# Two of the four weight sums of a seven-product matrix multiply move to a GpSimd DMA, and all eight chunks use seven products

## The chip, the cores and the metric

The kernel runs on one core of one Trainium2 chip. The metric is the device time of one execution in microseconds (us); runs are compared by their medians. The core has a matrix engine (TensorE: PE for its matmuls, PEld for its weight loads), a vector engine (VectorE, DVE), a scalar engine (ScalarE, ACT), GpSimd (POOL), and SyncE (SP), which here only issues DMAs. Each engine works through its own instructions in order and waits at an instruction until the semaphores it needs have been set.

## The reference

Two layers work on 256 tokens of width 2048 in float32: a recurrent block with a feed-forward network (FFN), then a block of sliding-window attention with an FFN. The change is in the FFN:

```python
D_FF = ((8 * D_MODEL // 3 + 255) // 256) * 256     # 5632

def swiglu_ffn(x, g, w_in, w_out):
    h = rms_norm(x, g)
    gate, up = jnp.split(h @ w_in, 2, axis=-1)
    return x + (jax.nn.silu(gate) * up) @ w_out
```

## The kernel before, in words

**Jobs.** All weights come from DRAM in tiles of 128 x 1024 float32 (512 KB), 704 of them. One tile is one job: SP loads it into a buffer `raw` (four of them, used in turn), it is split into a rounded part `hi` and a remainder `lo` (four buffers each), and PE multiplies with both parts: three matmuls (high by high, low by high, high by low) stand for one float32 product. ACT makes `hi` (L363), DVE makes `lo` = `raw` - `hi` (L364). `stream` (L385) writes the program job by job: at job i it issues the load of job i + LD (4), the split of job i + LC (3), and the matmuls of job i. Between, it lets background tasks write their instructions, as long as counters of DVE's and ACT's work (`run_bg`) leave room. At build time a scheduler of the framework puts each engine's instructions in their final order, so they can stand in another order than they were written.

**The FFN's first multiply** has 22 groups of eight jobs (chunks of 256 rows of the weights) per layer. Groups 0 to 3 and the odd ones from 5 to 21 are ordinary: 24 matmuls of 256 columns a job. Groups 4, 6, ..., 20 (`FAST`, nine per layer, 18 in all) are fast groups: a chunk is a 2 x 2 block product, done with seven block products in place of eight, 21 matmuls in place of 24 (`fast`, L588). For that, sums of blocks of the weights are needed: `mix` (L366) makes `hi` and `lo` of three of the four 256-column blocks (L374, L379) and, in a buffer `d` of 128 x 1024, four sums: two by one DVE subtraction over 512 columns (L375), one more by L376, one more by L377. `d` is then split into `mh` (ACT, L378) and `ml` (DVE, L380). Seven of the eight chunks are done so (`PAIRS`); chunk 3 is done by `plain` (L573) with 24 matmuls and an ordinary split. `joined` (L742) puts the partial products of a fast group together, applies silu, and multiplies; `turn` transposes the result on PE (L765).

**What is kept.** A gated result is 128 x 512 (256 KB); 22 per layer stay in SBUF until `split` (L676) divides them into high and low parts for the FFN's second multiply. Working buffers of 128 x 1024 come from a pool of 37 (`WORK`); part of x is parked in DRAM during the FFN (`park`, `fetch`).

Of the kernel before, what the change touches and what calls it, by code (L numbers as in the profile page):

```python
# [17 lines left out]
P = 128  # L18
# [31 lines left out]
class Trunk:  # L50
    LD = 4
    LC = 3
# [12 lines left out]
    FAST = tuple(range(4, 21, 2))  # L65
    PAIRS = (0, 1, 2, 4, 5, 6, 7)
    EVEN = (0, 4)
    OWED = 9000.0
    BUSY = 780.0
    WORK = 37  # L70
    NEAR = 7
    MORE = 2800.0
    WARM = 30
# [3 lines left out]
    def __init__(self, ctx, tc, dram):  # L77
# [12 lines left out]
        const.tile([P, PAD], F32, name="pad")  # L90
        self.raw = [const.tile([P, 1024], F32, name=f"raw{i}") for i in range(4)]
        self.hi = [const.tile([P, 1024], F32R, name=f"hi{i}") for i in range(4)]
# [25 lines left out]
        self.started = False  # L118
        self.jobs = []
        self.mixed = {}  # L120
        self.pend = deque()
# [214 lines left out]
    def load(self, i):  # L336
        dma = self.nc.sync.dma_start
        raw, src = self.raw[i % 4], self.jobs[i][0]
        if i == 0:

            self.nc.scalar.dma_start(self.x[0][:, 0:2, :], self.d["x"][:, 0:2, :])
            self.nc.scalar.dma_start(self.par, self.d["par"])
            for h in range(2):
                dma(raw[:, 512 * h:512 * h + 512], src[:, 512 * h:512 * h + 512])
            dma(self.x[0][:, 2:4, :], self.d["x"][:, 2:4, :])
        else:
            dma(raw, src)
            if i in self.XLOAD:
                n = self.XLOAD[i]
                dma(self.x[n], self.d["x"][:, 4 * n:4 * n + 4, :])  # L350
                self.got = n
        if i == 4:
            dma(self.con, self.d["con"])

    def split(self, i):
        raw, hi, lo = self.raw[i % 4], self.hi[i % 4], self.lo[i % 4]
        if self.jobs[i][2]:
# [3 lines left out]
        for c in range(0, 1024, n):  # L361
            q = slice(c, c + n)
            self.nc.scalar.activation(hi[:, q], raw[:, q], AF.Copy)  # L363
            self.nc.vector.tensor_tensor(lo[:, q], raw[:, q], hi[:, q].bitcast(F32), ALU.subtract)  # L364

    def mix(self, i, raw, hi, lo):  # L366

        act, tt = self.nc.scalar.activation, self.nc.vector.tensor_tensor
        d = self.double(F32, True)
        near = self.jobs[i][2] == 1  # L370
        mh, ml = self.double(near=near), self.double(near=near)
        two = lambda ap: ap.rearrange("p (a c) -> p a c", c=T)
        q = slice(T, 4 * T)
        act(hi[:, q], raw[:, q], AF.Copy)  # L374
        tt(two(d[:, 0:2 * T]), two(raw[:, T:3 * T]), raw[:, 0:T].unsqueeze(1).to_broadcast([P, 2, T]), ALU.subtract)  # L375
        tt(d[:, 2 * T:3 * T], raw[:, 2 * T:3 * T], d[:, 0:T], ALU.add)  # L376
# [8 lines left out]
    def stream(self):  # L385
        n = len(self.jobs)
        for i in range(-self.LD, n):
            self.tick = 2 * i
            if i + self.LD < n:
                self.load(i + self.LD)  # L390
            if 0 <= i + self.LC < n:
                self.split(i + self.LC)
# [169 lines left out]
    def fast_group(self, src, xn, mx, g, done, final):  # L562
# [3 lines left out]

        def put(h, x, w, n=1):
            b = h // 2
            nc.tensor.matmul(st["ps"][b][:, h % 2 * T:(h % 2 + n) * T], x, w, start=b not in st["begun"], stop=True,  # L569
                             skip_group_check=True)  # L570
            st["begun"].add(b)

        def plain(c, hi, lo):  # L573

            x2 = [self.need(xn[2 * c + kt]) for kt in range(2)]
            wide = []
            for kt in range(2):
                for i in range(2):
                    xh, xl = (x2[kt][:, q * T + i * P:q * T + i * P + P] for q in range(2))
                    for x, w in ((xh, hi), (xl, hi), (xh, lo)):  # L580
                        wide.append((2 - 2 * i, x, w[:, kt * 2 * T:kt * 2 * T + 2 * T]))
            todo = [(h + e, x, w[:, e * T:e * T + T]) for h, x, w in wide for e in range(2)]
            for k, t in enumerate(todo):
                if k == len(todo) // 2:
                    self.half_tick()
                put(*t)

# [24 lines left out]
        for c in range(8):  # L612
            def mm(hi, lo, c=c):
                if c == 0:
                    st["ps"] = self.bank4()
                if c == self.EVEN[1]:
                    self.flush()
                (fast if c in self.PAIRS else plain)(c, hi, lo)
                if c == 7:
                    done(st["ps"])  # L620
            self.jobs.append((src(c), mm, (c in self.PAIRS) + (c in self.EVEN)))

# [5 lines left out]
    def ffn(self, l, xs, r, gains, rn, col, out=None):  # L628
# [47 lines left out]
        def split():  # L676
            for p in range(NH // 2):
                while not raws[p].ready:
                    yield 1
# [13 lines left out]
        def raw(g, s):  # L693
            raws[g].ap = s
            raws[g].ready = True

        for g in range(NH // 2):
# [44 lines left out]
            def joined(q, g=g):  # L742
# [6 lines left out]
                self.tt(two(part(1, 2)), two(at(6, 2)), twice(part(0)), ALU.add)  # L749
                self.tt(part(0), at(7), part(1), ALU.add)  # L750
                self.tt(c[:, 0:2 * T], at(0, 2), part(0, 2), ALU.add)
                self.tt(c[:, 2 * T:4 * T], at(2, 2), part(2, 2), ALU.add)
# [654 lines left out]
```

## Time and profile before

| | us |
|---|---|
| median of three runs (1970.23 to 1973.72) | 1971.62 |
| the profiled execution, its own time | 1970.22 |
| its span | 1968.4 |
| an ordinary group beside a fast one: 192 matmuls | 21.76 |
| the fast group after it: 171 matmuls and 4 transposes | 20.02 |

The span is what the profiler saw from the first to the last instruction; 1.8 us of the execution lie around it. Durations in a view are of one instruction from its start to its end; on one engine the next often starts a little before. A view of waits names the engine that waits, and behind the arrow what ended the wait. A view of windows gives for a stretch of time each engine's busy time, the granted clock, the share of time in which the 16 DMA engines moved packets, and GB/s.

### The profile page before, as it was taken

How to read it: one execution, taken by the hardware profiler on the slowest of the kernel's cores; microseconds unless marked ns; L12 is line 12 of the kernel's file. 1: busy time of each engine (PE TensorE's matmuls, PEld its weight loads, DVE VectorE, ACT ScalarE, POOL GpSimd, SP SyncE). 2: the span in 40 equal slices, each digit the busy share in tenths (PEclk: the TensorE clock that was granted, in tenths of full speed). 3: DMA queues.
4: the chain of work that ended last, by engine and by line, in shares of the span. 5: the costliest groups of instructions: out<-in, count | busy, mean ns of one | idle time of the engine just before them, and what ended most of it. 6: DMA issues, size and time to landing. Idle time of an engine off the chain costs nothing. (4 is left out here: it accounts for less than half of the span.)

```text
span 1968.4 us, 40256 instructions
## 1 busy us (share of the span) xinstructions
PE 1960.3 (100%) x16518; PEld 1920.3 (98%) x16518; DVE 1541.0 (78%) x2477; ACT 1144.2 (58%) x1672; POOL 0.2 (0%) x4
## 2 busy tenths in 40 slices
PE   9999999999999999999999999999999999999999
PEld 9999999999999999999998789999999999999999
DVE  7999868999899997554667776699899988954443
ACT  6798756555555566444566675565555555744442
POOL 0000000000000000000000000000000000000000
PEclk9999999999999999999999999999999999999999
DMA  8555665566656657656554335656666665666663
GB/s 281 183 192 177 218 215 193 176 212 205 211 196 204 204 200 244 196 187 202 194 182 145 123 119 170 208 186 201 201 204 203 203 214 196 235 204 204 205 204 128
DMA packets 107321, 384.97 MB, mean 196 GB/s; under 512 B 11904, under 2 KB 14080, under 8 KB 107136
## 3 DMA queue, kind: packets, MB, share of 16 engines
q1 hardware_dynamic: 106848, 381.99, 58.7%
q8 instruction: 129, 2.11, 0.4%
q14 instruction: 56, 0.46, 0.1%
q10 hardware_dynamic: 288, 0.40, 0.1%
HBM read 376.06 MB, written 6.29 MB: 194 GB/s over the span
## 5 line engine op out<-in xcount | busy, mean ns | idle before, releaser
L411 PE MATMUL b<-s,hi 128*128 128x256 f32 (+1 forms) x7958 | 1060.0, 280 | 1.4 <-ACT s L135 1.2
L411 PEld LDWEIGHTS b<-s,hi 128*128 128x128 f32 x7958 | 987.5, 188 | 13.2 <-ACT s L135 2.1
L364 DVE TENSOR_TENSOR lo<-raw,hi 128x1024 fp32r<-128x1024 f32 (+1 forms) x579 | 702.6, 1220 | 320.2 <-ACT hi L363 312.7
L363 ACT ACTIVATE hi<-raw 128x1024 fp32r<-128x1024 f32 (+1 forms) x579 | 608.1, 1056 | 469.8 <-PE b L411 405.4
L411 PE MATMUL b<-s,lo 128*128 128x256 f32 x4096 | 607.0, 276 | 0.0
L411 PEld LDWEIGHTS b<-s,lo 128*128 128x128 f32 x4096 | 530.3, 188 | 0.2
L378 ACT ACTIVATE s<-s 128x1024 fp32r<-128x1024 f32 x126 | 131.8, 1058 | 189.1 <-DVE s L377 189.0
L569 PE MATMUL b<-s,s 128*128 128x256 f32 x1512 | 195.9, 279 | 0.0
L569 PEld LDWEIGHTS b<-s,s 128*128 128x128 f32 x1512 | 183.0, 189 | 0.0
L569 PE MATMUL b<-hi,s 128*128 128x256 f32 x1044 | 178.0, 277 | 0.0
L380 DVE TENSOR_TENSOR s<-s,s 128x1024 fp32r<-128x1024 f32 x126 | 153.7, 1220 | 6.0 <-ACT s L378 5.9
L569 PEld LDWEIGHTS b<-hi,s 128*128 128x128 f32 x1044 | 152.3, 188 | 0.0
L569 PE MATMUL b<-lo,s 128*128 128x256 f32 x522 | 132.5, 276 | 0.0
L375 DVE TENSOR_TENSOR s<-raw 128x512 f32<-128x512 f32 x126 | 86.6, 687 | 43.5 <-DMA raw<-in_ffn_in 43.5
L379 DVE TENSOR_TENSOR lo<-raw,hi 128x768 fp32r<-128x768 f32 x126 | 118.6, 952 | 0.0
L135 ACT ACTIVATE s<-s 128x512 fp32r<-128x512 f32 (+3 forms) x176 | 87.6, 525 | 48.8 <-DVE s L144 36.9
L374 ACT ACTIVATE hi<-raw 128x768 fp32r<-128x768 f32 x126 | 102.1, 832 | 9.1 <-ACT s L378 4.9
L569 PEld LDWEIGHTS b<-lo,s 128*128 128x128 f32 x522 | 92.7, 188 | 0.0
L1295 PE MATMUL b<-hi,s 128*128 128x512 f32 x256 | 83.5, 406 | 0.0
L144 DVE TENSOR_TENSOR s<-s,s 128x512 fp32r<-128x512 f32 (+2 forms) x143 | 75.3, 557 | 3.9 <-ACT s L135 3.9
L135 ACT ACTIVATE s<-b 128x256 fp32r<-128x256 f32 (+4 forms) x134 | 58.9, 468 | 26.3 <-PE b L1269 6.7
L144 DVE TENSOR_TENSOR s<-b,s 128x512 f32<-128x512 f32 (+3 forms) x126 | 63.4, 533 | 5.3 <-ACT s L135 4.0
(115 smaller groups left out, 1112.9 us busy)
## 6 DMA issues: line engine op xcount, KB each, us to landing
raw<-in_ffn_in SPq DMA_DIRECT2D x352, 512.0 KB, 3.4
raw<-in_ffn_out SPq DMA_DIRECT2D x176, 512.0 KB, 4.2
raw<-in_lru_in SPq DMA_DIRECT2D x63, 512.0 KB, 4.0
raw<-in_lru_out SPq DMA_DIRECT2D x32, 512.0 KB, 3.3
raw<-in_w_q SPq DMA_DIRECT2D x32, 512.0 KB, 3.2
raw<-in_w_o SPq DMA_DIRECT2D x32, 512.0 KB, 3.6
raw<-in_gate SPq DMA_DIRECT2D x8, 512.0 KB, 4.1
away<-s SPq DMA_DIRECT2D x8, 512.0 KB, 3.2
```

Source lines behind the costliest of these rows:

```text
L135: self.nc.scalar.activation(out, in_, func, **kw)
L144: self.nc.vector.tensor_tensor(out, a, b, op)
L363: self.nc.scalar.activation(hi[:, q], raw[:, q], AF.Copy)
L364: self.nc.vector.tensor_tensor(lo[:, q], raw[:, q], hi[:, q].bitcast(F32), ALU.subtract)
L374: act(hi[:, q], raw[:, q], AF.Copy)
L375: tt(two(d[:, 0:2 * T]), two(raw[:, T:3 * T]), raw[:, 0:T].unsqueeze(1).to_broadcast([P, 2, T]), ALU.subtract)
L378: act(mh[:, :], d[:, :], AF.Copy)
L379: tt(lo[:, q], raw[:, q], hi[:, q].bitcast(F32), ALU.subtract)
L380: self.mark = tt(ml[:, :], d[:, :], mh[:, :].bitcast(F32), ALU.subtract)
L411: self.nc.tensor.matmul(ps[f][:, 0:c1 - c0], w, x2[k][:, c0:c1], start=f not in begun, stop=last and all(q[1] != f for q in todo[n + 1:]))
L569: nc.tensor.matmul(st["ps"][b][:, h % 2 * T:(h % 2 + n) * T], x, w, start=b not in st["begun"], stop=True, skip_group_check=True)
L1295: nc.tensor.matmul(st[g][b][:, :], x, q, start=c + kt == 0 and x is xh and q is wh, stop=c == 7 and kt == 1 and q is wl)
```

## The change

- A fifth `raw` buffer (`LP` = 5), and loads written six jobs ahead (`LD` = 6).
- `PAIRS` holds all eight chunks, `plain` is gone, so each fast group has 168 matmuls.
- Two of the four sums are no longer made by DVE's L375. A new step `two_sums`, written five jobs ahead of the matmuls and so two jobs ahead of `mix`, has ACT write the negated first block twice into `d`, and GpSimd issue a DMA that adds 512 columns of `raw` onto it.
- `joined` does without the sum that only `plain` needed.
- Gated results 8 to 13 of each layer are stored to DRAM by SP and loaded again when `split` is six results ahead of their use: 12 stores and 12 loads of 256 KB in all.
- The pool has 36 working buffers in place of 37; the planner's entry for a mixed chunk's DVE work, `MORE`, is 2200 in place of 2800.

```diff
-    LD = 4
+    LD = 6
+    LP = 5
...
-    PAIRS = (0, 1, 2, 4, 5, 6, 7)
+    PAIRS = tuple(range(8))
     EVEN = (0, 4)
+    ASIDE = tuple(range(8, 14))
...
-    WORK = 37
+    WORK = 36
     NEAR = 7
-    MORE = 2800.0
+    MORE = 2200.0
...
+    def two_sums(self, i):
+
+        if not self.jobs[i][2]:
+            return
+        raw, d = self.raw[i % self.LP], self.double(F32)
+        two = lambda ap: ap.rearrange("p (a c) -> p a c", c=T)
+        self.a(two(d[:, 0:2 * T]), raw[:, 0:T].unsqueeze(1).to_broadcast([P, 2, T]), scale=-1.0)
+        self.nc.gpsimd.dma_start(d[:, 0:2 * T], raw[:, T:3 * T], accum_op=ALU.add)
+        self.begun[i] = d
+
     def mix(self, i, raw, hi, lo):
 
         act, tt = self.nc.scalar.activation, self.nc.vector.tensor_tensor
-        d = self.double(F32, True)
+        d = self.begun.pop(i)
         near = self.jobs[i][2] == 1
         mh, ml = self.double(near=near), self.double(near=near)
-        two = lambda ap: ap.rearrange("p (a c) -> p a c", c=T)
         q = slice(T, 4 * T)
         act(hi[:, q], raw[:, q], AF.Copy)
-        tt(two(d[:, 0:2 * T]), two(raw[:, T:3 * T]), raw[:, 0:T].unsqueeze(1).to_broadcast([P, 2, T]), ALU.subtract)
         tt(d[:, 2 * T:3 * T], raw[:, 2 * T:3 * T], d[:, 0:T], ALU.add)
...
             if i + self.LD < n:
                 self.load(i + self.LD)
+            if 0 <= i + self.LP < n:
+                self.two_sums(i + self.LP)
             if 0 <= i + self.LC < n:
                 self.split(i + self.LC)
...
-                (fast if c in self.PAIRS else plain)(c, hi, lo)
+                fast(c, hi, lo)
...
         def split():
             for p in range(NH // 2):
+                if p + 6 in self.ASIDE:
+                    q = p + 6
+                    s = raws[q].ap = self.slot(F32)
+                    nc.sync.dma_start(s, self.away[l, q][:, :])
+                    raws[q].ready = True
...
         def raw(g, s):
             raws[g].ap = s
             raws[g].ready = True
+            q = g - 2
+            if q in self.ASIDE:
+                away = self.away[l, q] = self.dram.tile([P, 2 * T], F32, name=f"aside{l}_{q}")
+                nc.sync.dma_start(away[:, :], raws[q].ap)
+                self.free(raws[q].ap)
+                raws[q].ready = False
...
                 self.tt(two(part(1, 2)), two(at(6, 2)), twice(part(0)), ALU.add)
-                self.tt(part(0), at(7), part(1), ALU.add)
-                self.tt(c[:, 0:2 * T], at(0, 2), part(0, 2), ALU.add)
+                self.tt(c[:, 0:T], at(7), part(1), ALU.add)
+                self.tt(c[:, T:2 * T], at(1), part(1), ALU.add)
```

What this does to the order of instructions is shown at three places of the second layer, each in one pair of an ordinary and a fast group. The number behind `raw` names one of its buffers (73 to 76 before, 73 to 77 now), that behind `hi` and `lo` one of theirs; `s` with a number is one use of a working buffer.

ACT before, from the middle of an ordinary group on: the splits of the ordinary jobs (`hi` of 1024 columns, L363), then of the fast group's first chunks (`hi` of 768 columns, L374), between them the `mh` (`s`<-`s`, L378).

```order
L363 ACTIVATE hi_78<-raw_74 128x1024
L363 ACTIVATE hi_79<-raw_75 128x1024
L363 ACTIVATE hi_80<-raw_76 128x1024
L378 ACTIVATE s_15559<-s_15558 128x1024
L374 ACTIVATE hi_77<-raw_73 128x768
L378 ACTIVATE s_15594<-s_15593 128x1024
L374 ACTIVATE hi_78<-raw_74 128x768
L378 ACTIVATE s_15629<-s_15628 128x1024
L374 ACTIVATE hi_79<-raw_75 128x768
L135 ACTIVATE h_92<-b_146 128x256
L363 ACTIVATE hi_80<-raw_76 128x1024
L135 ACTIVATE h_91<-b_147 128x256
```

ACT now, at the same place: the negated copies (`s`<-`raw`, L138) of the first four chunks, the ordinary splits (L366), the first three `mh` (L389) and the `hi` of the first two chunks (L386).

```order
L138 ACTIVATE s_15666<-raw_76 128x512
L366 ACTIVATE hi_79<-raw_73 128x1024
L366 ACTIVATE hi_80<-raw_74 128x1024
L138 ACTIVATE s_15696<-raw_77 128x512
L389 ACTIVATE s_15729<-s_15666 128x1024
L138 ACTIVATE s_15726<-raw_73 128x512
L366 ACTIVATE hi_81<-raw_75 128x1024
L138 ACTIVATE s_15762<-raw_74 128x512
L386 ACTIVATE hi_78<-raw_76 128x768
L389 ACTIVATE s_15765<-s_15696 128x1024
L389 ACTIVATE s_15801<-s_15726 128x1024
L386 ACTIVATE hi_79<-raw_77 128x768
```

The copy of a chunk stands two to three jobs ahead of its `hi`, and the third chunk's copy stands behind the first chunk's `mh`.

DVE before, at that place: the sums of the first three chunks (L375, L376, L377), two ordinary `lo` (L364), the first `lo` of the fast group (L379) and two `ml` (L380).

```order
L375 TENSOR_TENSOR s_15558<-raw_73 128x512
L364 TENSOR_TENSOR lo_83<-raw_75,hi_79 128x1024
L376 TENSOR_TENSOR s_15558<-raw_73,s_15558 128x256
L377 TENSOR_TENSOR s_15558<-raw_73,s_15558 128x256
L375 TENSOR_TENSOR s_15593<-raw_74 128x512
L376 TENSOR_TENSOR s_15593<-raw_74,s_15593 128x256
L364 TENSOR_TENSOR lo_84<-raw_76,hi_80 128x1024
L380 TENSOR_TENSOR s_15560<-s_15558,s_15559 128x1024
L377 TENSOR_TENSOR s_15593<-raw_74,s_15593 128x256
L375 TENSOR_TENSOR s_15628<-raw_75 128x512
L379 TENSOR_TENSOR lo_81<-raw_73,hi_77 128x768
L380 TENSOR_TENSOR s_15595<-s_15593,s_15594 128x1024
```

DVE now: L387 and L388 are the two sums that are left to it, L367 and L390 the `lo` of ordinary and fast jobs, L391 the `ml`.

```order
L387 TENSOR_TENSOR s_15666<-raw_76,s_15666 128x256
L388 TENSOR_TENSOR s_15666<-raw_76,s_15666 128x256
L367 TENSOR_TENSOR lo_84<-raw_74,hi_80 128x1024
L391 TENSOR_TENSOR s_15730<-s_15666,s_15729 128x1024
L387 TENSOR_TENSOR s_15696<-raw_77,s_15696 128x256
L367 TENSOR_TENSOR lo_85<-raw_75,hi_81 128x1024
L388 TENSOR_TENSOR s_15696<-raw_77,s_15696 128x256
L387 TENSOR_TENSOR s_15726<-raw_73,s_15726 128x256
L388 TENSOR_TENSOR s_15726<-raw_73,s_15726 128x256
L390 TENSOR_TENSOR lo_82<-raw_76,hi_78 128x768
L391 TENSOR_TENSOR s_15766<-s_15696,s_15765 128x1024
L391 TENSOR_TENSOR s_15802<-s_15726,s_15801 128x1024
```

The 512-column subtraction is gone from each chunk. L387 now waits for the GpSimd DMA of its chunk, and the `lo` of an ordinary job (L367) can stand behind it.

DVE before, in the second half of the same fast group: sums, `lo` and `ml` of its last four chunks.

```order
L380 TENSOR_TENSOR s_15693<-s_15691,s_15692 128x1024
L379 TENSOR_TENSOR lo_81<-raw_73,hi_77 128x768
L379 TENSOR_TENSOR lo_82<-raw_74,hi_78 128x768
L380 TENSOR_TENSOR s_15725<-s_15723,s_15724 128x1024
L375 TENSOR_TENSOR s_15755<-raw_75 128x512
L379 TENSOR_TENSOR lo_83<-raw_75,hi_79 128x768
L376 TENSOR_TENSOR s_15755<-raw_75,s_15755 128x256
L375 TENSOR_TENSOR s_15790<-raw_76 128x512
L377 TENSOR_TENSOR s_15755<-raw_75,s_15755 128x256
L376 TENSOR_TENSOR s_15790<-raw_76,s_15790 128x256
L377 TENSOR_TENSOR s_15790<-raw_76,s_15790 128x256
L380 TENSOR_TENSOR s_15757<-s_15755,s_15756 128x1024
```

DVE now, in the second half of the fast group, from the sixth chunk's L387 on (buffer raw_76, which the first chunk had before it); the two L147 are halves of an earlier ordinary group's gated result.

```order
L387 TENSOR_TENSOR s_15838<-raw_76,s_15838 128x256
L147 TENSOR_TENSOR s_15648<-h_93,b_144 128x256
L388 TENSOR_TENSOR s_15838<-raw_76,s_15838 128x256
L390 TENSOR_TENSOR lo_85<-raw_74,hi_81 128x768
L147 TENSOR_TENSOR s_15648<-h_91,b_145 128x256
L391 TENSOR_TENSOR s_15875<-s_15798,s_15874 128x1024
L390 TENSOR_TENSOR lo_82<-raw_75,hi_78 128x768
L387 TENSOR_TENSOR s_15871<-raw_77,s_15871 128x256
L388 TENSOR_TENSOR s_15871<-raw_77,s_15871 128x256
L390 TENSOR_TENSOR lo_83<-raw_76,hi_79 128x768
L391 TENSOR_TENSOR s_15908<-s_15838,s_15907 128x1024
L390 TENSOR_TENSOR lo_84<-raw_77,hi_80 128x768
```

Five more rows end the group: the seventh chunk's `ml`, then L387, `lo`, L388 and `ml` of the eighth. Behind them stand four L367 in a row, the first four jobs of the next ordinary group, the fourth of them from raw_77, the buffer that is loaded next with the first chunk of the next fast group. The fourth chunk's `lo` (from raw_74) now stands behind the sixth chunk's sums, and so behind a wait for the sixth chunk's DMA.

More of the change, by code (lines that the diff above doesn't have):

```diff
@@ L90, in __init__ @@
         const.tile([P, PAD], F32, name="pad")
-        self.raw = [const.tile([P, 1024], F32, name=f"raw{i}") for i in range(4)]
+        self.raw = [const.tile([P, 1024], F32, name=f"raw{i}") for i in range(self.LP)]
         self.hi = [const.tile([P, 1024], F32R, name=f"hi{i}") for i in range(4)]
@@ L119, in __init__ @@
         self.jobs = []
+        self.begun = {}
         self.mixed = {}
@@ L337, in load @@
         dma = self.nc.sync.dma_start
-        raw, src = self.raw[i % 4], self.jobs[i][0]
+        raw, src = self.raw[i % self.LP], self.jobs[i][0]
         if i == 0:
@@ L355, in split @@
     def split(self, i):
-        raw, hi, lo = self.raw[i % 4], self.hi[i % 4], self.lo[i % 4]
+        raw, hi, lo = self.raw[i % self.LP], self.hi[i % 4], self.lo[i % 4]
         if self.jobs[i][2]:
@@ L565, in fast_group, with put @@
         st = {"begun": set()}
-        def put(h, x, w, n=1):
+        def put(h, x, w):
             b = h // 2
-            nc.tensor.matmul(st["ps"][b][:, h % 2 * T:(h % 2 + n) * T], x, w, start=b not in st["begun"], stop=True,
+            nc.tensor.matmul(st["ps"][b][:, h % 2 * T:h % 2 * T + T], x, w, start=b not in st["begun"], stop=True,
                              skip_group_check=True)
             st["begun"].add(b)
[L573 to L586, printed above, removed]
         def fast(c, hi, lo):
@@ L617, in mm @@
                     self.flush()
-                (fast if c in self.PAIRS else plain)(c, hi, lo)
+                fast(c, hi, lo)
                 if c == 7:
                     done(st["ps"])
-            self.jobs.append((src(c), mm, (c in self.PAIRS) + (c in self.EVEN)))
+            self.jobs.append((src(c), mm, 1 + (c in self.EVEN)))
     def flush(self):
```

## The prediction

> **What bounds the kernel now.** I read the page's list of busy times first, then the chain that ended last in one pair of groups, then the stage of the fast groups by windows.
>
> ```profile
> span 1968.4 us, 40256 instructions
> PE 1960.3 (100%) x16518; PEld 1920.3 (98%) x16518; DVE 1541.0 (78%) x2477; ACT 1144.2 (58%) x1672; POOL 0.2 (0%) x4
> ...
> 1369.61 21.76 PE b L411 x192
> 1391.37 9.96 PE b L569 x87
> 1401.33 0.44 PE b L765 x4
> 1401.77 9.62 PE b L569 x84
> ...
> 1391.37:1703.80 312.43, 312.43 (x2746) 312.43 (x2746) 286.95 (x396) 183.11 (x220) 0.00 (x0) 1.00 0.61 203
> ...
> DVE s L375 <- DMA raw<-in_ffn_in: 16.1, 16, 2.1
> ```
>
> PE is idle for 8.1 us in all. In a pair, PE's own work is the whole chain: 192 matmuls in 21.76 us, then 171 in 9.96 + 9.62 us and 0.44 for four transposes, 41.77 us a pair. The window from the second pair's fast group to the end of the stage holds 7.5 pairs: PE busy throughout, at the full granted clock (1.00). But DVE is busy 286.95 of 312.43 us, 38.3 us a pair, and waited 16.1 us more, 2.1 a pair, for weights. So PE is the bound by a narrow margin: the stage has two engines near their limit. That settles the reading: what comes off PE counts in full, as long as DVE and its suppliers keep up.
>
> **What PE loses.** Chunk 3 of each fast group goes from 24 matmuls to 21, and the order of the program has 54 matmuls fewer (3 x 18). One is (9.96 + 9.62) / 171 = 0.1145 us, so 54 x 0.1145 = **6.2 us**. Nothing else on PE changes but a few places of single small matmuls.
>
> **What DVE and ACT gain or lose.**
>
> ```profile
> L364 DVE TENSOR_TENSOR lo<-raw,hi 128x1024 fp32r<-128x1024 f32 x577 | 701.3, 1222 | 316.3 <-ACT hi L363 308.9 <-PE b L569 4.4
> L380 DVE TENSOR_TENSOR s<-s,s 128x1024 fp32r<-128x1024 f32 x126 | 153.7, 1220 | 6.0 <-ACT s L378 5.9
> L379 DVE TENSOR_TENSOR lo<-raw,hi 128x768 fp32r<-128x768 f32 x126 | 118.6, 952 | 0.0
> L375 DVE TENSOR_TENSOR s<-raw 128x512 f32<-128x512 f32 x126 | 86.6, 687 | 43.5 <-DMA raw<-in_ffn_in 43.5
> L377 DVE TENSOR_TENSOR s<-raw,s 128x256 f32<-128x256 f32 x126 | 53.1, 421 | 1.7
> L144 DVE TENSOR_TENSOR s<-b,s 128x512 f32<-128x512 f32 x54 | 35.4, 684 | 0.5
> ...
> L363 ACT ACTIVATE hi<-raw 128x1024 fp32r<-128x1024 f32 x577 | 606.8, 1057 | 468.0 <-PE b L411 405.4 <-PE b L1295 15.6 <-DMA raw<-in_ffn_in 13.2
> L378 ACT ACTIVATE s<-s 128x1024 fp32r<-128x1024 f32 x126 | 131.8, 1058 | 189.1 <-DVE s L377 189.0
> L374 ACT ACTIVATE hi<-raw 128x768 fp32r<-128x768 f32 x126 | 102.1, 832 | 9.1 <-ACT s L378 4.9 <-ACT hi L374 3.4 <-PE b L411 0.4
> L135 ACT ACTIVATE s<-s 128x512 fp32r<-128x512 f32 x74 | 44.9, 624 | 23.3 <-DVE s L144 16.2 <-DVE s L148 6.6
> ```
>
> Per pair DVE loses seven L375 (7 x 0.687 = 4.8 us), and a 512-column sum of `joined` becomes one of 256 (0.26). Chunk 3 turns from one L364 (1.22) into 0.95 + 1.22 + 2 x 0.42 = 3.01, which costs 1.8. Net -3.3: 35.0 us of work in a pair that PE would run in 41.4. So DVE may idle 6.4 us a pair. ACT gets eight negated copies of 512 columns (I take L135's 0.62, the same size) and 0.83 us for chunk 3: 24.4 us a pair become 30.2, hidden as long as the copies do not stall it.
>
> **What takes L375's place.** The trace has no DMA issued by GpSimd and none that adds. Let D be the time from the end of the negated copy to the moment at which L387 may start.
>
> ```profile
> DMA to landing us min/median/max: 3.1/3.3/4.9
> s<-away SPq DMA_DIRECT2D x8, 512.0 KB, 6.6
> s<-in_x SPq DMA_DIRECT2D x3, 512.0 KB, 7.4
> s<-in_x ACTq DMA_DIRECT2D x1, 256.0 KB, 4.1
> out_y<-s SPq DMA_DIRECT2D x16, 128.0 KB, 3.6
> ```
>
> The first row is of 16 weight loads of the stage (512 KB, SP's queue), from issue to landing. A quarter of that size took 3.6 us elsewhere, so most of it does not go with size. Ends for D: 3.1 (the quickest load of the stage) and 7.4 (three large loads at the program's start). I take the nearest row, the stage's 3.3, plus 0.2 for two handovers between engines: **D = 3.5**. The Trainium skill (Collectives: The Full Stack, "Stop ④", on why ReduceScatter is half of AllGather) says that an adding DMA reads two sources per element written. By it this 256 KB sum reads 512 KB, as much as such a load; no run here shows it.
>
> Does D reach PE? I follow one round through the new order, from the last `lo` that frees raw for a fast group's first chunk to the same place a pair later. Four L364 in a row took 4.62 us, so a DVE step counts 0.08 less than its duration.
>
> ```profile
> 1408.84 4.62 DVE L364 TENSOR_TENSOR lo<-raw,hi 128x1024 fp32r<-128x1024 f32 x4
> ```
>
> - load of the first chunk 3.3, its copy 0.55, D, its L387 and L388 0.68, its `mh` on ACT 1.06; behind that in ACT's order the third chunk's copy 0.55: 6.1 + D
> - D, the third chunk's two sums 0.68, the first chunk's `lo` 0.87, which frees raw for the sixth chunk; load 3.3, copy 0.55: 5.4 + D
> - D, then DVE from the sixth chunk's L387 to the eighth's `ml`: six sums 2.04, five `lo` 4.35, four `ml` 4.56, two L144 0.66, one `mh` to wait for 1.06: 12.7 + D
> - four ordinary `lo` 4.6; some eight handovers of 0.1, 0.8
>
> Together **29.6 + 3 D**. With D = 3.5 that is 40.1 us, under PE's 41.4: the round has 1.3 us to spare and PE does not wait. It becomes the bound at D = 3.9, and the gain of 0.34 us a pair is used up at D = 4.06. Each 0.1 us beyond costs 0.3 us x 18 = 5.4 us. The other waits sit beside this round: ACT's copies need only their load, and each sum starts two jobs ahead of its use, 4.8 us at PE's pace, more than D.
>
> **DMA load.**
>
> ```profile
> 1391.37:1411.38 20.01, 20.01 (x177) 20.01 (x177) 19.61 (x28) 12.70 (x17) 0.00 (x0) 1.00 0.54 179
> 1411.38:1433.14 21.76, 21.76 (x195) 21.76 (x194) 18.88 (x27) 10.86 (x13) 0.00 (x0) 1.00 0.68 224
> 10.00:20.00 10.00, 10.00 (x87) 10.00 (x86) 9.83 (x22) 8.96 (x22) 0.00 (x0) 1.00 1.03 412
> ```
>
> Eight sums of 256 KB are 2.1 MB a pair, 51 GB/s over 41.4 us if they count once, 101 if twice, upon 203. The queues once carried 412 GB/s, so the mean fits; in bursts, loads may land later (rival 2).
>
> **Aside tiles, pool and loads.** 24 transfers of 256 KB add 6.3 MB to 385 and 24 issues to SP's queue, in front of weight loads. The stores wait for results of two groups earlier. The reloads wait for PE to finish with the buffers they take, as the four fetches did before; behind them stand the loads of the last ordinary group. Cover: in ordinary groups ACT's `hi` waits 405.4 us for PE and 13.2 us for weights, so loads arrive early there; without it, one late load costs at most its 3.3 us, once per layer. I put this at 0, bounds -2 (the fifth buffer takes away waits, but PE's 8.1 us of idle time are elsewhere) to +7. The program's start moves one pair of background operations ahead of a half tile's split, which PE needs only after its first 12 products: 0.
>
> **Sum.** 1970.22 - 6.2 = 1964.0 us for a profiled execution. The median of before lies 1.4 above that execution, so **1965.4 us**.
>
> **Rivals.**
>
> 1. *The sum comes late* (slower). D is above 4.06 and the round above replaces PE as the bound. For it: DVE's order has an ordinary `lo` behind L387, ACT's has the copies in front of `hi`, so one late sum stops both; GpSimd's share of D is unseen. Against: 6.4 us of DVE slack a pair. At D = 4.5 the round is 43.1 us, 1.3 above 41.77, x 18 = 24: 1996 us. At the stage's latest landing, D = 4.9: 44.3, +46, 2017 us. At 7.4 it is 51.8, +180, 2152 us, which nothing at these DMA loads suggests.
> 2. *The sums lengthen the loads* (same). Both draw on the same 16 engines. If loads land in 4.0 in place of 3.3 and D is 3.6, the round is 29.6 + 1.4 + 10.8 = 41.8: the gain is gone and the time 1970 to 1972 us.
> 3. *GpSimd is held off by DVE* (slower). Mechanism: while one of DVE's two-input operations runs, GpSimd cannot prepare the transfer and waits out up to 1.2 us. D = 4.7, the round 43.7, +1.9 x 18 = 35: 2007 us. For it: nearly all of DVE's work in the stage is such TENSOR_TENSORs, and DVE is busy 92%. The Trainium skill (SBUF — State Buffer, "Who interferes with whom") says that two-input operations contend only with a GpSimd instruction that reads SBUF, and warns of operations in two-port modes. By it rival 3 needs that preparing reads SBUF; no trace here shows GpSimd at work.
>
> That the change does not do what it says is excluded for PE: the order has the 54 matmuls fewer.
>
> **Chances.** Forecast 0.52; rival 1 0.25, rival 2 0.15, rival 3 0.08. The margin of the round, 0.4 us of D, is small against what is unknown of D, so I give the forecast no more. Its own range is 1962.5 to 1967.5 (bounds of the aside tiles, and the margin partly used). The range of all is 1962.5 to 1996: above it lie about half of rivals 1 and 3, 0.17. A measurement of this kernel can tell about 0.2%, 3.9 us, from no change: faster 0.52, same 0.15, slower 0.33.
>
> **What would show it.** Right: PE 54 matmuls fewer; a fast group of 168 matmuls in 19.7 us; no wait on PE or PEld by `lo` or `s` in the stage; DVE's wait for weights gone, its waits for the added sums under 6 us a pair; issue to landing of the sums 3.3 to 3.7. Wrong: PE waits at the eighth chunk's `ml` or the next group's `lo`, pairs longer than 41.8 us (rival 1; with GpSimd's start delayed until DVE's operations end, rival 3); weight loads at 4 us or more (rival 2).

## The result, and the profile after

| | before | after |
|---|---|---|
| median, us | 1970.92 | 2055.66 |
| range of four runs each | 1969.74 to 1973.72 | 2052.42 to 2061.73 |
| span of the profiled execution | 1968.4 | 2050.6 |
| the 18 fast groups together, by the first matmul of each group | 359.1 | 438.4 |

The ratio is 1.0431, with a 95% interval of 1.0404 to 1.0459: the changed kernel is slower by about 85 us. The fast groups hold 79.3 of the 82.2 us by which the span grew. They now take 22.1 to 27.2 us, where 19.6 to 20.0 stood before and 19.7 was forecast; an ordinary group nearly always still takes 21.8 us, and the stretch between the two layers' stages is the same to 0.1 us.

From the page of the changed kernel: span, busy times, the DMA queues (packets, MB, share of 16 engines), groups of instructions, and issues with their median time to landing.

```profile
span 2050.6 us, 40877 instructions
PE 1989.5 (97%) x16464; PEld 1937.3 (94%) x16464; DVE 1498.1 (73%) x2415; ACT 1230.7 (60%) x1836; POOL 124.6 (6%) x148
...
q1 hardware_dynamic: 110304, 388.29, 56.6%
q0 software_dynamic: 20736, 37.76, 11.0%
...
L376 POOL DMA_DIRECT2D s<-raw x144 | 124.4, 864 | 1649.1 <-ACT s L138 1490.3
...
raw<-in_ffn_in SPq DMA_DIRECT2D x352, 512.0 KB, 4.2
...
s<-raw POOLq DMA_DIRECT2D x144, 256.0 KB, 4.0
```

PE has its 54 matmuls fewer (16464) and yet 61 us of idle time, where it had 8; its busy time grew as well, by 29 us, with the stalls and with a granted clock of 0.98 in the stage (below). DVE is less busy than before. The added DMA lands 4.0 us after its issue in the median, and the weight loads 4.2. The next view is that of line L376, the GpSimd DMA: its instruction's duration (ns, min/median/max), then the time from issue to landing.

```profile
L376 POOL DMA_DIRECT2D s<-raw x144: 859/859/1002, 372.4 to 1773.2; - x144
DMA to landing us min/median/max: 3.2/4.0/7.0
```

The windows of seven pairs in the second layer:

```profile
1440.54:1761.73 321.19, 302.56 (x2550) 298.19 (x2549) 245.06 (x335) 197.12 (x257) 47.83 (x56) 0.98 0.84 233
```

A pair takes 321.19 / 7 = 45.9 us (41.77 before). DVE has 245.06 / 7 = 35.0 us of work in it, as forecast, so 10.9 us of idle time, and the DMA share rose from 0.61 to 0.84. The waits say where:

```profile
ACT s L138 <- DMA raw<-in_ffn_in: 151.7, 92, 4.1
DVE s L387 <- DMA s<-raw: 103.0, 61, 6.1
...
PEld b L582 <- DVE lo L390: 43.9, 36, 3.0
PE b L582 <- DVE lo L390: 36.4, 31, 2.8
```

L387 waits 103.0 us for added sums, up to 6.1 at a time; the copies on ACT (L138) wait 151.7 us for weights. PE waits most for `lo` of the chunks (L390), not for the eighth chunk's `ml`. The chain of waits over the nine fast groups of the second layer, by line, shares of 393.1 us:

```profile
by line: PE b L582 21.7%; DMA raw<-in_ffn_in 19.7%; DMA s<-raw 18.8%; issue 10.5%; PE b L424 8.6%; DVE lo L367 7.1%; DVE lo L390 3.6%; ACT hi L366 2.1%; DVE s L387 1.8%; DVE s L388 1.6%; ACT s L389 1.4%; PE b L774 0.9%; DVE s L391 0.7%; ACT
```

PE was the whole chain before; it holds 31% of it now. Weight loads hold 19.7% and the added sums 18.8%, 8.6 and 8.2 us a fast group. One round of it, from a `lo` that frees the raw buffer of a fast group's third chunk to the same place a pair later (start, duration, what; "issue" is time for which nothing is shown):

```profile
1564.78 1.24 DVE lo L367
1566.03 3.20 DMA raw<-in_ffn_in
...
1569.30 1.07 issue
1570.38 5.87 DMA s<-raw
...
1576.28 0.43 DVE s L387
...
1583.69 4.54 DMA raw<-in_ffn_in
...
1588.32 0.64 ACT s L138
1588.96 0.35 issue
1589.30 6.97 DMA s<-raw
...
1602.51 2.35 DVE lo L367 x2
...
1604.89 6.16 DMA raw<-in_ffn_in
...
1611.08 0.04 ACT s L138
...
1611.62 1.05 ACT hi L366
...
1612.70 1.24 DVE lo L367
1613.95 3.38 DMA raw<-in_ffn_in
```

The round is 1613.95 - 1566.03 = 47.9 us. In it are three weight loads (3.20 + 4.54 + 6.16 = 13.9) and two added sums (5.87 + 6.97 = 12.8), each with about 0.4 us of GpSimd's start (0.35 behind the second copy). Counted off in SP's order, the loads are those of the third chunk, the eighth and the next fast group's first. The forecast's round went from the first chunk's load through that chunk's own sum. Here ACT's negated copy of the first chunk waits for its load, behind that copy in ACT's order stands an ordinary `hi`, and its `lo` frees the third chunk's buffer: the first chunk's sum drops out, and the third chunk's load, which the forecast had beside the round, comes in. This is the longest of the six rounds in this chain, which take 44.4 to 47.9 us; four of the six pass three loads, and they pass one or two sums, most of them also some of PE's matmuls.

### The profile page after: what moved, and what is told of

The parts are those of the page before. It is cut to its first block, busy times and chain, and to the rows that moved or that the text cites. A ratio compares the mean times of both kernels' runs of the same rounds, so it can differ in the third digit from the quotient of the medians.

```text
span 2050.6 us, 40877 instructions
## 1 busy us (share of the span) xinstructions
PE 1989.5 (97%) x16464; PEld 1937.3 (94%) x16464; DVE 1498.1 (73%) x2415; ACT 1230.7 (60%) x1836; POOL 124.6 (6%) x148
## 3 DMA queue, kind: packets, MB, share of 16 engines
q0 software_dynamic: 20736, 37.76, 11.0%
## 5 line engine op out<-in xcount | busy, mean ns | idle before, releaser
L367 DVE TENSOR_TENSOR lo<-raw,hi 128x1024 fp32r<-128x1024 f32 (+1 forms) x561 | 680.4, 1222 | 352.1 <-ACT hi L366 349.4
L366 ACT ACTIVATE hi<-raw 128x1024 fp32r<-128x1024 f32 (+1 forms) x561 | 584.7, 1053 | 385.2 <-PE b L424 345.2
L582 PE MATMUL b<-s,s 128*128 128x256 f32 x1728 | 235.7, 287 | 3.9 <-DVE s L391 2.2
L582 PEld LDWEIGHTS b<-s,s 128*128 128x128 f32 x1728 | 220.0, 196 | 5.1 <-DVE s L391 3.3
L376 POOL DMA_DIRECT2D s<-raw x144 | 124.4, 864 | 1649.1 <-ACT s L138 1490.3
L389 ACT ACTIVATE s<-s 128x1024 fp32r<-128x1024 f32 x144 | 151.6, 1055 | 106.4 <-DVE s L388 90.4
L391 DVE TENSOR_TENSOR s<-s,s 128x1024 fp32r<-128x1024 f32 x144 | 174.4, 1221 | 20.8 <-ACT s L389 20.1
L138 ACT ACTIVATE s<-raw 128x512 f32<-128x512 f32 x144 | 90.5, 628 | 153.9 <-DMA raw<-in_ffn_in 151.7
L582 PE MATMUL b<-hi,s 128*128 128x256 f32 x864 | 160.1, 283 | 12.1 <-ACT hi L386 12.1
L390 DVE TENSOR_TENSOR lo<-raw,hi 128x768 fp32r<-128x768 f32 x144 | 137.4, 954 | 18.4 <-ACT hi L386 18.4
L582 PEld LDWEIGHTS b<-hi,s 128*128 128x128 f32 x864 | 132.9, 191 | 15.4 <-ACT hi L386 15.3
L387 DVE TENSOR_TENSOR s<-raw,s 128x256 f32<-128x256 f32 x144 | 60.9, 423 | 103.3 <-DMA s<-raw 103.0
L138 ACT ACTIVATE s<-s 128x512 fp32r<-128x512 f32 (+3 forms) x180 | 89.6, 525 | 70.8 <-DVE s L147 61.1
L386 ACT ACTIVATE hi<-raw 128x768 fp32r<-128x768 f32 x144 | 118.1, 830 | 0.0
L147 DVE TENSOR_TENSOR s<-s,s 128x512 fp32r<-128x512 f32 (+2 forms) x146 | 77.3, 561 | 4.5 <-ACT s L138 4.5
```

The lines of the kernel that those rows point to most:

```text
L138: self.nc.scalar.activation(out, in_, func, **kw)
L147: self.nc.vector.tensor_tensor(out, a, b, op)
L376: self.nc.gpsimd.dma_start(d[:, 0:2 * T], raw[:, T:3 * T], accum_op=ALU.add)
L389: act(mh[:, :], d[:, :], AF.Copy)
L390: tt(lo[:, q], raw[:, q], hi[:, q].bitcast(F32), ALU.subtract)
L391: self.mark = tt(ml[:, :], d[:, :], mh[:, :].bitcast(F32), ALU.subtract)
```

## The experiments

Sixteen kernels ran. Where an interval is given, the kernel was timed in three rounds against the kernel before; the others ran once. Edits are against the changed kernel unless another is named.

**1. Without the DMA: DVE makes the two sums again** (`MORE` stays at 2200).

```diff
 def mix(self, i, raw, hi, lo):
-    d = self.begun.pop(i)
+    d = self.double(F32, True)
+    tt(two(d[:, 0:2 * T]), two(raw[:, T:3 * T]), raw[:, 0:T]..., ALU.subtract)
...
-            if 0 <= i + self.LP < n:
-                self.two_sums(i + self.LP)
```

> The changed kernel with the two sums back on DVE (no negated copy, no GpSimd DMA); fifth raw buffer, eight chunks by seven products, aside tiles, smaller pool kept. Theory A (the time from the negated copy to the sum's landing, taken three times in each round of a pair of groups, is the whole loss): the stalls go; DVE has 35.0 + 8 x 0.69 = 40.5 us of work in a pair that PE runs in 41.4, so 1963 to 1975 us, and PE idles under 20 us. Theory B (the loss comes from the other parts: loads behind the aside transfers, the smaller pool, the loads written six ahead): at least 2030 us.

Measured: 2009.63 us, ratio 1.0197 (1.0180 to 1.0214). Missed by both theories. The chain of waits of this kernel from 1440 to 1700 us, by line (L388 is the subtraction over 512 columns, L389 and L390 the other sums, L392 and L393 `lo` and `ml`):

```profile
by line: issue 17.0%; PE b L424 14.9%; DVE lo L367 13.4%; DVE s L388 11.7%; DVE s L393 10.2%; DVE lo L392 8.6%; DVE s L389 7.1%; ACT s L391 7.0%; DVE s L390 5.2%; PE b L582 3.3%; DVE s L147 1.6%; DVEq L367 0.1%; DVEq L388 0.0%
```

57.8% of it is DVE and 18.2% PE: with eight mixed chunks and all sums, DVE is the bound. The same showed in the kernel before with nothing changed but `PAIRS` (all eight) and `joined`:

```diff
-    PAIRS = (0, 1, 2, 4, 5, 6, 7)
+    PAIRS = tuple(range(8))
```

> The kernel before with all eight chunks by seven products, nothing else: the sums stay on DVE, four raw buffers, no aside tiles. By PE alone it gains 6.2 us: 1964 us. Theory A (DVE was nearly full): DVE's 38.3 us a pair become 40.5, and the waits for weights of 2.1 us stay, together above PE's 41.4: 1968 to 1990 us. If it comes out at 1964 to 1966, DVE had more room than I read, and the rest of the change was not needed for the 54 matmuls.

Measured: 2031.96 us, 1.0313 (1.0298 to 1.0329), slower as theory A says, but far above its range. So the eighth chunk needs DVE relieved; that aim of the change was sound.

**2. What the transfer itself costs.** First the DMA copies and adds nothing, then it adds 16 columns only.

```diff
-        self.nc.gpsimd.dma_start(d[:, 0:2 * T], raw[:, T:3 * T], accum_op=ALU.add)
+        self.nc.gpsimd.dma_start(d[:, 0:2 * T], raw[:, T:3 * T])
```

> The changed kernel, but the GpSimd DMA copies its 512 columns and adds nothing, so the two sums are left out. If adding is what makes the transfer slow (two reads for each element written), issue to landing falls from 4.0 by 0.6 us or more, and with it the round by 1.8 us or more a pair: 2020 us or less. If GpSimd's own part and the shared engines make it, landing stays within 0.3 us of 4.0 and the time at 2035 to 2060 us.

```diff
-        self.nc.gpsimd.dma_start(d[:, 0:2 * T], raw[:, T:3 * T], accum_op=ALU.add)
+        self.nc.gpsimd.dma_start(d[:, 0:16], raw[:, T:T + 16], accum_op=ALU.add)
```

> The changed kernel, but the GpSimd DMA adds 16 columns of each of the 128 rows in place of 512, so nearly all of the two sums is left out. Theory A by a fixed part (GpSimd's preparation and the way there and back): landing stays at 3.5 to 4 us and the time at 2010 us or more. Theory A by bytes and by contention with the weight loads: landing falls to 2.5 to 3 us, weight loads fall back from 4.2 to 3.4 us, the round to some 39 us, below PE's 41.4: 1964 to 1975 us.

Measured: 2018.16 us for the copy, 2000.76 for the short add. The views of line L376 in the two kernels, the copying one first:

```profile
L376 POOL DMA_DIRECT2D s<-raw x144: 536/536/670, 372.6 to 1739.0; - x144
DMA to landing us min/median/max: 2.2/3.2/5.9
```

```profile
L376 POOL DMA_DIRECT2D s<-raw x144: 859/859/1002, 371.5 to 1722.5; - x144
DMA to landing us min/median/max: 2.0/2.6/5.8
```

Adding in place of copying costs 0.8 us of landing and some 37 us of the kernel's time, as the first of the two forecasts for the copy has it; nearly all bytes taken away bring 55 us. Some 30 us are left even so, and neither theory had that. The order of instructions hardly differs among these three kernels: the scheduler gave the copying one the order of the changed one on every engine, and the one with the short adds nearly so.

**3. More lead.** Loads a job earlier and a sixth buffer, so that each sum starts three jobs ahead of its use:

```diff
-    LD = 6
-    LP = 5
+    LD = 7
+    LP = 6
...
-    WORK = 36
+    WORK = 35
```

> The changed kernel with a sixth raw buffer, loads seven ahead and the negated copies six ahead (three jobs before the mix), pool of 35. Theory A (a round of latencies: weight load, copy, sum, spread over five jobs of lead): a sixth job of lead takes about 2.4 us out of each round, pairs of 45.9 us become 43.5, 2005 to 2020 us. Theory C (the shared DMA engines, 0.84 busy in the stage, are the bound): the time stays at 2040 us or more.

Measured: 2066.58 us, 1.0481 (1.0459 to 1.0502). No gain: only theory C's range held. That does not show the DMA engines to be the bound: their share is 0.84 in this kernel and in the changed one, but 0.65 with the short adds, which still lose 30 us. Why the earlier start does not help was not taken apart. Nor does another order on ACT help, each copy behind the ordinary or mixed `hi` written before it (`self.high` is that `hi`):

```diff
-            if 0 <= i + self.LP < n:
-                self.two_sums(i + self.LP)
             if 0 <= i + self.LC < n:
                 self.split(i + self.LC)
+            if 0 <= i + self.LP < n:
+                self.two_sums(i + self.LP)
...
+        with self.tc.issue_after(self.high.ins):
+            self.a(two(d[:, 0:2 * T]), raw[:, 0:T]..., scale=-1.0)
```

> The changed kernel with the negated copy of job i+5 put behind the high part of job i+3 on ACT, so it holds up no ordinary split that stands before. If the copies that wait for weights in front of ordinary splits are a main part of the loss: ACT's waits for weights at L138 fall from 152 us to under 80 and the time to 2030 us or less. If the sums' latency alone counts: later copies make later sums, 2056 us or more.

Measured: 2094.24 us, worse. The copies' waits for weights fell from 151.7 us to 1.3, so it isn't enough to take these waits from in front of a `hi`. The copy that holds up a `hi` is one side of a trade: copies that come later make later sums, and these landed 5.6 us after their issue in the median, where it was 4.0.

**4. The other parts of the change alone.** The sums on DVE as in 1, chunk 3 ordinary again (24 matmuls, `plain` and `joined` as before), `MORE` at 2800; the fifth buffer, loads six ahead, the aside tiles and the pool of 36 stay.

```diff
-    PAIRS = tuple(range(8))
+    PAIRS = (0, 1, 2, 4, 5, 6, 7)
...
-                fast(c, hi, lo)
+                (fast if c in self.PAIRS else plain)(c, hi, lo)
```

> The changed kernel without its two gains: the sums on DVE and chunk 3 by 24 matmuls again, so DVE and PE have the work of before; fifth raw buffer, loads six ahead, aside tiles and the smaller pool kept. Theory A (these parts cost nothing, the loss is the sums' latency and the weight loads that the copies hold): 1968 to 1974 us. Theory B (they cost by themselves): 1985 us or more, the difference to 1970 being their price.

Measured: 1972.62 us, 1.0003 (0.9993 to 1.0012). These parts cost nothing, as forecast.

**5. The DMA for some chunks only**, chunks 3, 6 and 7; DVE makes the sums of the other five.

```diff
+    VIA = (3, 6, 7)
...
+        if not via:
+            tt(two(d[:, 0:2 * T]), two(raw[:, T:3 * T]), raw[:, 0:T]..., ALU.subtract)
```

> The changed kernel with copy and GpSimd sum only for chunks 3, 6 and 7 of each fast group; the other five have both sums on DVE, as before. Theory A: DVE is relieved by 3 x 0.69 = 2.1 us a pair against e1_dve_sums (43.5 us a pair), to 41.4, just PE's own; these three sums have 5 us or more until they are needed, so nothing waits for them: 1964 to 1980 us, below e1's 2010 in any case. Theory C (any GpSimd sum disturbs loads and order): 2010 us or more.

Measured: 2008.19 us, 1.0173 (1.0149 to 1.0196). Missed: far above theory A's range, just under theory C's. The three sums landed after 4.6 us in the median, and five subtractions are back on DVE; how much is due to each was not taken apart.

**6. Which part of the change carries the loss.** Chunk 3 ordinary again (`plain` and `joined` as before), the DMA kept for the seven others:

```diff
-    PAIRS = tuple(range(8))
+    PAIRS = (0, 1, 2, 4, 5, 6, 7)
...
-                fast(c, hi, lo)
+                (fast if c in self.PAIRS else plain)(c, hi, lo)
```

> The changed kernel with chunk 3 ordinary again (24 matmuls, one split), but the added DMA sums kept for the seven mixed chunks. The runs so far leave two theories for the loss. Theory A (the eighth chunk tips it): seven chunks leave DVE and ACT slack in the middle of a group, and the sums then come in time: 1966 to 1978 us, near the kernel before, sums landing at 4.0. Theory B (the sums by DMA are late in any case): pairs stay above 43.5 us and the time is 2010 us or more. A value between (1985 to 2005) means that each has a share of its own.

And the other way round, all eight chunks mixed but no copy and no DMA:

```diff
-        self.a(two(d[:, 0:2 * T]), raw[:, 0:T]..., scale=-1.0)
-        self.nc.gpsimd.dma_start(d[:, 0:2 * T], raw[:, T:3 * T], accum_op=ALU.add)
+        self.nc.gpsimd.memset(d[:, 0:2 * T], 0.0)
```

> The changed kernel with the two sums left out: GpSimd writes zeros into the two blocks of d, ACT makes no negated copy and no DMA adds anything; all eight chunks are mixed, DVE has the same 35.0 us of work a pair. Theory A (the eighth chunk's own work in DVE's and ACT's order tips it): 1990 to 2005 us, as with the short adds (2001). Theory B (copy and DMA, whatever their length, are the whole loss): the forecast's 1962 to 1968 us.

Measured: seven chunks with the DMA 2062.61 us, 1.0471 (1.0448 to 1.0494); eight without copy and DMA 1964.30 us, 0.9965 (0.9952 to 0.9977). That settles theory B: the eighth chunk isn't the cause, the supply of the two sums is, with the order of instructions that comes with it (see 7). The chain of waits of the second kernel, in one pair (L581 is a fast group's matmul, L423 an ordinary one's, L773 the transposes):

```profile
1408.04 21.76 PE b L423 x192
1429.80 9.62 PE b L581 x84
1439.42 0.44 PE b L773 x4
1439.86 9.61 PE b L581 x84
```

19.67 us for 168 matmuls and four transposes: PE alone is the chain again.

**7. Copy, DMA, or delay.** The copies alone, the DMA line left out:

```diff
-        self.nc.gpsimd.dma_start(d[:, 0:2 * T], raw[:, T:3 * T], accum_op=ALU.add)
```

> The changed kernel with the negated copies on ACT kept and GpSimd's DMA left out: the two blocks of d hold the negated first block alone. Theory C (the copies in ACT's order, each waiting for its load and holding up the high parts behind it, make up what was left with the short adds): 1990 to 2005 us. Theory D (only the time from the copy to the sum counts): 1962 to 1968 us, as with GpSimd's zeros (1964.3).

Measured: 1965.00 us, 0.9970 (0.9959 to 0.9980). The copies on ACT cost nothing by themselves. The DMA alone, as a plain copy:

```diff
-        self.a(two(d[:, 0:2 * T]), raw[:, 0:T]..., scale=-1.0)
-        self.nc.gpsimd.dma_start(d[:, 0:2 * T], raw[:, T:3 * T], accum_op=ALU.add)
+        self.nc.gpsimd.dma_start(d[:, 0:2 * T], raw[:, T:3 * T])
```

> The changed kernel without the negated copies: GpSimd's DMA copies two blocks of raw into d, starts when the weights have landed, and adds nothing (the subtraction is left out). Theory C: without the copies the time falls from 2018 (copies and plain DMA) to 1964 to 1980 us. Theory D: the DMA's landing of 3.2 us is still behind the load, about 0.6 us earlier than with the copy: 1990 to 2010 us.

Measured: 2040.60 us. More than with the copies (2018), which no theory had; its fast groups take 19.7 to 22.1 us or 25.0 to 27.5, none between. The sums come earlier behind their load here, and the kernel is slower: the time from load to sum alone does not order these kernels. Why it is worse without the copies was not found. Last, the copy and a delay without any DMA, of six and of four writes of zeros:

```diff
-        self.nc.gpsimd.dma_start(d[:, 0:2 * T], raw[:, T:3 * T], accum_op=ALU.add)
+        for _ in range(6):
+            self.nc.gpsimd.memset(d[:, 0:2 * T], 0.0)
```

> The changed kernel with the copy kept and, in place of the DMA, six writes of zeros by GpSimd, one behind the other, 6 x 0.53 = 3.2 us: a fixed delay after the copy of about the median landing of the short adds (2.6) to the plain copies (3.2), with no DMA traffic and no spread; the sums are left out. If the mean delay alone makes the loss: 1995 to 2020 us. If the spread of the landings and the DMA load make it: 1962 to 1972 us.

> The copy and four writes of zeros, 2.1 us, in place of six (3.2 us, 1990); the sums are left out. If the delay enters the round of a pair three times and the rest of the round is 32.6 us in place of the forecast's 29.6, the round is 39.5 us, under PE's 41.4, and the time is 1963 to 1968 us. If each delay costs something from zero on (in proportion to 3.2 us): 1978 to 1984 us.

Measured: six writes 1990.18 us, 1.0101 (1.0086 to 1.0116); four writes 1971.28 us, 1.0002 (0.9993 to 1.0012). Both lie between the two ranges given. The chain of the kernel with six writes, from the load of a fast group's first chunk to the same place a pair later:

```profile
1642.95 5.40 DMA raw<-in_ffn_in
...
1648.38 0.64 ACT s L138
1649.02 0.05 issue
1649.07 0.54 POOL s L377
...
1651.99 0.54 POOL s L377
...
1652.55 0.44 DVE s L388
...
1653.35 1.23 DVE lo L367
...
1654.60 3.12 DMA raw<-in_ffn_in
...
1660.13 3.58 DMA raw<-in_ffn_in
...
1672.16 9.29 PE b L583 x81
...
1682.79 2.35 DVE lo L367 x2
...
1685.17 5.52 DMA raw<-in_ffn_in
```

From this first chunk's copy to L388 it is 1652.55 - 1649.02 = 3.5 us, the very D that the forecast took. The round is 42.2 us all the same: three loads (12.1 us), and PE's own matmuls in it.

But the delay is that for the first chunk of a group, not for the others. GpSimd works in order, six writes last longer than the time between two copies, and the scheduler put writes of neighbouring chunks between one another. Of the group's 48 writes the last 32 stand behind one another without a gap:

```profile
1658.43 16.46 POOL L377 MEMSET s<- 128x512 f32 x32 [0.16 <-ACT s L138]
```

The eighth chunk's copy had ended at 1670.26, so its last write, at 1674.89, came 4.6 us later. The next table has the time from the end of a copy to the end of the chunk's last write or the landing of its DMA, worked out for each of the 144 chunks from the trace and the order of the program.

| behind the copy | delay, us: median (least to longest) | time, us |
|---|---|---|
| nothing | 0 | 1965.0 |
| four writes | 2.3 (2.3 to 4.2) | 1971.3 |
| six writes | 5.1 (3.5 to 7.3) | 1990.2 |
| DMA, adds 16 columns | 2.9 (2.3 to 6.1) | 2000.8 |
| DMA, copies | 3.6 (2.5 to 6.2) | 2018.2 |
| DMA, adds (the change) | 4.4 (3.6 to 7.4) | 2055.7 |

Among the three DMAs, whose kernels have the same order or nearly so, the time rises with the delay. Among the writes it rises too: 2.3 us already cost 6. But the six writes hold the sums up longer in the median than any DMA here does, and nearly as unevenly, and cost the least of the four. So neither the delay nor its spread is the whole price of the DMA. One thing that differs besides the DMA is the order: behind copies alone, zeros and writes the scheduler placed ACT's and DVE's instructions in another way, and with the six writes the fourth chunk's `lo` stands ahead of the sixth chunk's sums in all 18 fast groups, where it stands behind them in 16 in the changed kernel. How much is order, and how much the DMA's traffic, no run held apart.

**8. The sums without a DMA, on GpSimd itself**: written beside `mix`, and then five jobs ahead.

```diff
-        tt(two(d[:, 0:2 * T]), two(raw[:, T:3 * T]), raw[:, 0:T]..., ALU.subtract)
+        self.nc.gpsimd.tensor_tensor(two(d[:, 0:2 * T]), two(raw[:, T:3 * T]), raw[:, 0:T]..., ALU.subtract)
```

The first is against the kernel of 1; the second has this line in `two_sums`, in place of the copy and the DMA.

> All eight chunks, with the two sums made by one subtraction of GpSimd's own in place of a copy and an adding DMA. Theory B (latency of copy and DMA): GpSimd needs less than 2.5 us for 128x512 and nothing is loaded on the DMA engines, so 1964 to 1985 us. Theory A (eighth chunk): 1995 to 2015 us, as with DVE's sums (2010). If GpSimd takes over 4 us for one, it is itself late and the time is above 2030.

> The changed kernel, all of the sums computed, with one subtraction of GpSimd's own (1.30 us when undisturbed, 1.46 mean, in the run that put it beside the other sums) in the place of the copy and the adding DMA, written five jobs ahead like them. No copy, no DMA; the sums are there about 1.5 us after the load. If a delay under 2 us costs PE nothing: 1963 to 1968 us, faster than before. If GpSimd and DVE hold each other up where their subtractions meet (single DVE operations took 2.36 in place of 1.22 us there): 1985 us or more.

Measured: 2120.78 us, which no theory had with GpSimd at 1.46 us a subtraction, and early 2078.46 us, 1.0534 (1.0505 to 1.0564), as the second forecast says. The groups of the early one by line and shape (busy, mean ns of one):

```profile
L375 POOL TENSOR_TENSOR s<-raw 128x512 f32<-128x512 f32 x144 | 218.3, 1518 | 1583.2 <-DMA raw<-in_ffn_in 912.2 <-PE b L423 618.2 <-ACT hi L366 18.5
L390 DVE TENSOR_TENSOR s<-s,s 128x1024 fp32r<-128x1024 f32 x144 | 205.4, 1427 | 9.3 <-ACT s L388 8.6
...
L386 DVE TENSOR_TENSOR s<-raw,s 128x256 f32<-128x256 f32 x144 | 80.3, 559 | 62.7 <-POOL s L375 62.7
```

In the kernel of zeros the same `ml` and sum read:

```profile
L390 DVE TENSOR_TENSOR s<-s,s 128x1024 fp32r<-128x1024 f32 x144 | 175.8, 1222 | 4.0 <-ACT s L388 1.7
...
L386 DVE TENSOR_TENSOR s<-raw,s 128x256 f32<-128x256 f32 x144 | 60.4, 422 | 39.6 <-DMA raw<-in_ffn_in 38.1
```

1222 and 422 ns there, 1427 and 559 here. GpSimd's subtraction is quick enough by its least time (1.26 us; 2.40 at most), but it and DVE's work hold each other up. Whether that is the whole loss was not taken apart. No version that computes all sums beat the kernel before.

## Why the prediction was wrong, point by point

- **PE's part was right.** "54 x 0.1145 = 6.2 us" and the forecast median of 1965.4 came out at 1964.3 and 1965.0, once the two sums had no supply time (experiments 6 and 7); a fast group then takes the 19.7 us forecast. In the changed kernel the gain was there and was paid over.
- **DVE's part was right**: 35.0 us a pair. It isn't work that PE waits for but order: DVE is idle 10.9 us a pair and late all the same. "DVE may idle 6.4 us a pair" read a sum of durations as if the idle time could lie anywhere.
- **"D = 3.5" failed.** The median is 4.0 + 0.4 = 4.4 us, and the longest 7.4. The nearest row was a weight load by SP (3.3); a DMA that adds lands later. The chain takes late landings, 4.9 us in the mean (18.8% of 393.1 us for 15 sums), not the median.
- **"29.6 + 3 D ... becomes the bound at D = 3.9" failed, and this alone would have turned the sign.** With the short adds D is 2.9 us in the median, with the copying DMA 3.6. By the formula both rounds stay under PE's 41.4 us, yet the kernels take 2001 and 2018 us; a D of 2.3 already costs 6. The round has up to three weight loads and not two, because "ACT's copies need only their load" overlooked the ordinary `hi` behind the first chunk's copy; they take 3.1 to 6.2 us where 3.3 was counted; and in most rounds PE's matmuls lie in it as well. It passes one or two sums and not three, so the number of D was too high and the rest too low. How the loss divides between the delay, the order and the DMA's traffic stays open.
- **Aside tiles, pool, fifth buffer at 0: right** (ratio 1.0003).
- **Rival 1 was the right kind and priced too low**: 1996 us for D = 4.5, 2017 for 4.9. It used the same round: at the measured median of 4.4 that gives some 1990 us, where 2055.7 was measured.
- **Rival 2** named 4.0 us for the loads, and they take 4.2. Over the whole stage it is not the sums that do it: with the copies alone, no added transfer and no wait on PE, the stage's weight loads land as late, as their view there shows:

```profile
DMA to landing us min/median/max: 3.0/4.1/6.3
```

Of the fast groups' loads alone, which the round passes, the median is 3.3 us there and 3.9 in the changed kernel. It is 4.0 in the kernel of experiment 1 too, which has no such DMA, so this is not shown to be the sums' doing either.

- **Rival 3 shows no trace of itself.** GpSimd's DMA instruction took 859 ns in the median and at least, 1002 at most, among DVE's subtractions, and began 0.29 to 0.49 us behind its copy every time. The Trainium skill (SBUF — State Buffer, "Who interferes with whom") has two-input operations contend with a GpSimd instruction that reads SBUF; the trace agrees where GpSimd's own subtraction, which does read it, lengthened DVE's L386 from 422 to 559 ns.

## What to carry to other kernels

When work goes from a busy engine to a DMA, the question is not whether the engine then has time to spare but how long the round is in which the result is wanted: loads, splits and buffers that are given back all lie in it, and here 2.3 us more already cost 6. Walk such a round through the real order, count every load that an in-order engine waits for ahead of other work, and take landings from their upper half. A cheap test before building it is to leave the sum out and put delays in its place: nothing, four writes and six writes gave 1965, 1971 and 1990 us. Read from the trace which delays came out, and from the program whether the order stayed: here they told that a delay costs, and not how much the DMA would.

## What the runs showed of the hardware

- A DMA from SBUF to SBUF that adds 256 KB lands in 3.2 / 4.0 / 7.0 us (least, median, longest) in this stage, a copy of as much in 2.2 / 3.2 / 5.9, and an add of 16 columns (8 KB) still in 2.0 / 2.6 / 5.8. Its queue took 11.0% of the 16 engines' span against 4.9% for copies of the same 37.76 MB, as the row of the copying kernel shows. The Trainium skill (Collectives: The Full Stack, "Stop ④") says that an adding DMA reads two sources; the trace agrees, at 2.3 times the engine time (11.0% of 2050.6 us over 4.9% of that kernel's 2016 us).

```profile
q0 software_dynamic: 11520, 37.76, 4.9%
```

- GpSimd's instruction that issues the adding DMA took 0.86 us in the median, that of the copying one 0.54.
- GpSimd's subtraction of 128x512 took 1.26 us at best and 1.52 in the mean. DVE's busy time rose from 1501.1 us (zeros by GpSimd) to 1604.0 (subtractions by GpSimd) for the same 2415 instructions.
